# Routing rows normed early, experts gathered several at a time, a fifth raw buffer: one change to a two-layer decoder kernel

## The chip, the cores and the metric

The kernel runs on one core of a Trainium2 chip. The metric is the device time of one execution in microseconds (us). The engines are named as in the profile: PE is the matmul engine and PEld its weight loads, DVE the vector engine, ACT the scalar engine, POOL the GpSimd engine, and SP the engine that issues the DMAs. They run side by side and wait for each other by semaphores. PE's accumulators lie in PSUM, in eight banks of 128 x 512 floats.

## The reference

Two layers over 256 tokens of width 1024. Layer 0 is attention and a state space block followed by a dense feed-forward. Layer 1 is two kinds of attention followed by the part that the change touches, eight experts of which each token takes two:

```python
def moe_swiglu(h, router, w_gate, w_up, w_down):   # h: rms_norm(x, gain)
    logits = (t @ router).astype(jnp.float32)      # t: 256 x 1024, router: 1024 x 8
    top_val, top_idx = lax.top_k(logits, 2)
    top_w = jax.nn.softmax(top_val, axis=-1)
    ...   # out += gate of expert e * swiglu(t, w_gate[e], w_up[e], w_down[e])
```

`rms_norm` divides a row by its root mean square and multiplies by a gain for each column. `swiglu(h)` is `(silu(h @ gate) * (h @ up)) @ down`, with 2816 hidden columns.

## The kernel before

**Numbers in two halves.** Weights and activations are 32-bit floats. A matmul on the fast type (fp32r) keeps fewer digits, so `split` writes each 128 x 2048 weight tile `raw` as a rounded tile `wh` (ACT) and the rest `wl` (DVE, after ACT), and `mm3` (L513 to L517) issues three matmuls: high by high (L515), high by low (L516), low by high (L517).

**The order up to the routing's end** is made by `Recorder`: operations are recorded with their costs, planned over the engines under the number of buffers of each tile name (`RAW` for `raw`, 8 for PSUM), and then issued in that order. These instructions all carry line L326. `rec.late` marks operations of low urgency. After `rec.flush(...)` and `rec.on = False` the program is issued as it is written; those instructions carry L331.

**Routing.** For each of the two blocks b of 128 tokens, x3 (tile `xres`) is transposed by PE in pieces of 128 columns and multiplied by the router, in which the gain is folded (`rg`). The piece of x is the stationary operand and the 8 columns of the router are the moving one. x3 itself, not yet normed, is split into `xnh` and `xnl`. The logits give the two best experts by MAX8 and MAX_INDEX (`t8`, `i8`), the mask `m` and, with an exponential that needs the row scale `rows`, the weights `gate`. Two matmuls with triangular tables on `m` number the tokens of each expert (`posm`) and count them. The experts are then ordered by count: `poso` holds the positions in that order, `ids` the experts' numbers.

**Large and small.** The four fullest experts (`BIG = 4`; expert 0 is always the first) get 128 slots, the four others 64. `one_hots(p)` makes the one-hot tables of large expert p and small expert p. `gather` picks an expert's tokens out of xnh and xnl by multiplying with them, for 128 of the 1024 columns (index k) at a time. Four matmuls, of 128 + 64 = 192 columns where both experts are gathered together. The result is split into a tile pair `xb` (alternating between `fh` and `xg0`) for the large expert and kept whole in `xs` for the small. As the rows were not normed, `slot_scale` multiplies the tables with `rows` to get each slot's scale, used as `scale` in SiLU and in the product.

**Items.** The weights of an expert come in 11 chunks (`FC`) of three 1 MB units: gate and up, first half; gate and up, second half; down. A large chunk multiplies by `mm3`; a small one directly in 32 bits with the unsplit tile, two half arrays side by side. The list `items` starts with `LAG = 3` large chunks alone, then alternates large chunk g and small chunk g − 3, and ends with three small chunks alone. In item i, PE does the first gate and up unit of the item, transposes the hidden values of the item before, does the second unit, and then the down unit of the item before. The gather for large expert p + 1 and small expert p + 1 stands in the chunks c = 3 to 10 of expert p, one k in each; the tokens of small expert 0 are gathered in chunks 0 to 2 of expert 0.

**Loads.** `Stream` issues the units in order on SP, each into the next buffer that comes free: `RAW = 4` of the name `raw`, and `xres`, `xg0` (for loads up to `XG = 12`), `xg1`, `more` and `fl`. A buffer of a large unit is free when it has been split, one of a small unit when PE has used it. `st.ahead` splits up to `HL = 4` units ahead. Units of an expert other than the first need `ids`, which SP reads into a register.

Of the kernel before, what the change touches and what calls it, by code (L numbers as in the profile page):

```python
# [48 lines left out]
RAW = 4  # L49
# [3 lines left out]
XG = 12  # L53
BIG = 4
HALFP = 64
LAG = 3
PAIRED = 0.65
LATE, AFTER, HALF = 1, 2, 3
# [334 lines left out]
def kernel(ctx: ExitStack, tc: tile.TileContext, a, out: bass.AP):  # L393
# [379 lines left out]
    def ff_act(gu, scales, act=None):  # L773
        hs = []
        for b in range(len(gu)):
            si = tw(256)
            (act or tact)(si, gu[b][:, 0:256], AF.Silu, scale=scales[b])
            hh = tw(256)
            V.scalar_tensor_tensor(hh, gu[b][:, 256:512], scales[b], si, op0=OP.mult, op1=OP.mult)
            hs.append(hh)  # L780
        return hs
# [560 lines left out]
    rows, slots = mo([P, 2], "rows"), mo([P, 8], "slots")  # L1342
    for b in range(2):
        rx3 = rows[:, b:b + 1]
        lps = pa()
        for i in range(2):
# [24 lines left out]
        block_rstd(x3, b, rx3)  # L1371
# [9 lines left out]
        rec.late = 0  # L1381
    pp, pm = pa(), pa()
# [56 lines left out]
    def one_hots(p):  # L1439

        t = tw(dt=F32R).rearrange("p (b e s) -> p b e s", b=2, e=2)
        for b in range(2):
            one_hot(t[:, b, 0, :], (poso if p else posm)[:, b, p:p + 1])
            V.tensor_scalar(t[:, b, 1, :].rearrange("p (i s) -> p i s", i=2), bc(iota[:, None, 0:HALFP], [P, 2, HALFP]),
                            poso[:, b, BIG + p:BIG + p + 1], None, op0=OP.is_equal)
        return t

    oh = {0: one_hots(0)}


    def gather(k, ohs, xb=None, xs=None):

        lo, hi = 0 if xb else P, P + HALFP if xs is not None else P
        o = pa()[:, lo:hi]
        for i, src in enumerate((xnh, xnl)):
            for b in range(2):
                mmx(o, src[:, b, k * P:(k + 1) * P], ohs(b)[:, lo:hi], i + b == 0, i + b == 2)
        gain = k2("gf1k", k, k + 1)
        if xb:
            split_gain(xb[0][:, k], xb[1][:, k], o[:, 0:P], gain)  # L1460
        if xs is not None:
            S.activation(xs[:, k], o[:, P - lo:hi - lo], AF.Copy, scale=gain)

    def slot_scale(dst, ohs):

        sp, n = pa(), ohs.shape[2]
        for e in range(n):
            for b in range(2):
                mmx(sp[:, e:e + 1], ohs[:, b, e, :].bitcast(F32), rows[:, b:b + 1], b == 0, b == 1)
        V.tensor_copy(dst, sp[:, 0:n])  # L1470
# [30 lines left out]
    def large_tile(p):  # L1501
        t = mo([P, 2, 8, P], "xg0", F32R) if p % 2 else gtile([P, 2, 8, P], F32R, "fh")
        return t[:, 0], t[:, 1]

    def small_tile():
        return rec.tile(mo.pool, [P, 8, HALFP], F32, "mxs", 2, name="xs")
# [12 lines left out]
    def sm_act(gu, scale):  # L1519
        si, hh = tw(P), tw(P)  # L1520
        tact(si, gu[:, 0:P], AF.Silu, scale=scale)
        V.scalar_tensor_tensor(hh, gu[:, P:256], scale, si, op0=OP.mult, op1=OP.mult)
# [52 lines left out]
    xb, xs = {0: large_tile(0)}, {}  # L1575
    for k in range(8):
        gather(k, lambda b: oh[0][:, b].rearrange("p e s -> p (e s)"), xb[0])
    rec.late = AFTER
    slot_scale(slots[:, 0:2], oh[0])
    rec.late = 0  # L1580
    rec.flush([x3, oh[0], *xb[0], *st.tiles()])
    rec.on = False
    at.close()
    ov = out.rearrange("(b p) d -> p b d", p=P)
# [233 lines left out]
```

## Time and profile before

| what | value |
|---|---|
| median of 3 runs | 1165.53 us (1165.39 to 1167.24) |
| the profiled execution, its span | 1166.32 us, 1164.5 us |
| busy PE, PEld, DVE, ACT | 97%, 72%, 62%, 52% of the span |
| chain of work that ended last, by engine | PE 89%, DMA 5%, DVE 3%, ACT 1% |
| read from HBM | 345.95 MB, 298 GB/s over the span |
| split of weights on DVE, on ACT (128x2048, 90 each) | 206.4 us, 172.0 us |
| loads of expert units, issue to landing, median | 8.9 us into `raw` |

The first 450 us are the first layer and the second layer's attention; the routing ends at about 471 us and the experts fill the rest. PE is busy nearly always, and since its instructions overlap, a busy PE says little: what counts is how far apart matmuls start, and that is read from the timeline. DMA share and GB/s of a stretch say how near the loads are to their limit. In the chain of waits, each step is followed back to what released it. One execution is shown, and its stretches have different limits, so a saving is counted in the stretch where it is made.

### The profile page before, as it was taken

The page shows a single profiled execution, that of the slowest core. Times are in us where ns is not written, and L with a number is a line of the kernel's source. Part 1 is how long each engine was busy: PE and PEld are TensorE (multiplying, and loading weights), DVE is VectorE, ACT ScalarE, POOL GpSimd, SP SyncE. Part 2 cuts the span into 40 slices and gives each one's busy share as a digit, 9 for nine tenths or more (in the row PEclk, how much of TensorE's full clock was granted, in tenths as well). Part 3 has the DMA queues.
Part 4 walks back from the last instruction along what each step waited for, and adds up shares of the span by engine and source line. Part 5 has one row for each costly group of instructions (what it writes and reads, how often), then busy time and mean ns, then how long its engine had stood idle before and what let it go on. Part 6 is the DMA issues. An engine that isn't in the chain of part 4 may idle for free.

```text
span 1164.5 us, 16524 instructions
## 1 busy us (share of the span) xinstructions
PE 1133.4 (97%) x6143; PEld 833.2 (72%) x6143; DVE 720.7 (62%) x1185; ACT 601.2 (52%) x1016; POOL 28.7 (2%) x59
## 2 busy tenths in 40 slices
PE   6999999999999998999999999999999999999997
PEld 6887888888787777876666666666666666666663
DVE  5999954444399877665546565556565555565542
ACT  5768743444388565555445445554455444444331
POOL 1040000000300000000000000000000000000000
PEclk9999999999999998899999999999999999999999
DMA  9451565556344523489999999999999999999994
GB/s 348 154 190 73 183 214 186 188 182 220 112 160 163 194 73 145 176 330 356 401 414 415 419 377 409 395 423 420 393 419 389 420 382 406 411 410 420 415 415 156
DMA packets 52069, 348.13 MB, mean 299 GB/s; under 512 B 5904, under 2 KB 6032, under 8 KB 11536
## 3 DMA queue, kind: packets, MB, share of 16 engines
q1 hardware_dynamic: 51984, 347.02, 75.3%
q8 instruction: 50, 0.82, 0.3%
q14 instruction: 35, 0.29, 0.1%
HBM read 345.95 MB, written 1.05 MB: 298 GB/s over the span
## 4 chain that ended last, share of the span: by engine, by line
PE 89%; DMA 5%; DVE 3%; ACT 1%; issue 1%; SPq 0%; DVEq 0%; ACTq 0%
PE ps L331 24%; PE ps L515 19%; PE ps L517 18%; PE ps L516 18%; PE ps L326 10%; DMA raw<-in_moe_dram 2%; DMA fl<-in_moe_dram 1%; ACT wh L331 1%; DVE wl L326 1%; DMA raw<-in_w_dram 1%; DMA more<-in_moe_dram 1%; DVE wl L331 1%; DVE xres L331 0%; DVE tw L326 0%; DVE tw L331 0%
## 5 line engine op out<-in xcount | busy, mean ns | idle before, releaser
L331 DVE TENSOR_TENSOR wl<-raw,wh 128x2048 fp32r<-128x2048 f32 x90 | 206.4, 2293 | 156.5 <-ACT wh L331 156.5
L331 ACT ACTIVATE wh<-raw 128x2048 fp32r<-128x2048 f32 x90 | 172.0, 1911 | 110.3 <-DMA raw<-in_moe_dram 56.1
L515 PE MATMUL ps<-wh,fh 128*128 128x512 f32 (+2 forms) x544 | 220.4, 405 | 0.0
L516 PE MATMUL ps<-wl,fh 128*128 128x512 f32 (+2 forms) x544 | 211.4, 389 | 0.0
L331 ACT ACTIVATE tw<-ps 128x128 f32<-128x128 f32 (+2 forms) x114 | 43.6, 389 | 197.9 <-PE ps L331 195.9
L517 PE MATMUL ps<-wh,fl 128*128 128x512 f32 (+2 forms) x368 | 142.1, 386 | 0.0
L515 PEld LDWEIGHTS ps<-wh,fh 128*128 128x128 f32 x544 | 103.1, 189 | 20.0
L516 PEld LDWEIGHTS ps<-wl,fh 128*128 128x128 f32 x544 | 103.2, 190 | 17.6
L515 PE MATMUL ps<-wh,tw 128*128 128x512 f32 (+1 forms) x276 | 113.7, 412 | 0.7 <-ACT tw L326 0.7
L517 PE MATMUL ps<-wh,tw 128*128 128x512 f32 (+1 forms) x276 | 108.7, 394 | 0.0
L516 PE MATMUL ps<-wl,tw 128*128 128x512 f32 (+1 forms) x276 | 108.6, 394 | 0.0
L326 DVE TENSOR_TENSOR wl<-raw,wh 128x512 fp32r<-128x512 f32 (+1 forms) x149 | 98.4, 680 | 2.5 <-ACT wh L326 2.5
L331 DVE TENSOR_TENSOR tw<-ps,tw 128x256 fp32r<-128x256 f32 (+1 forms) x70 | 35.9, 521 | 97.5 <-ACT tw L331 97.4
L331 PE MATMUL ps<-raw,xs 128*64 128x256 f32 x720 | 87.2, 384 | 0.0
L326 ACT ACTIVATE wh<-raw 128x512 fp32r<-128x512 f32 (+1 forms) x130 | 74.8, 628 | 18.2 <-PE ps L517 10.0
L517 PEld LDWEIGHTS ps<-wh,fl 128*128 128x128 f32 x368 | 69.1, 188 | 14.6 <-DVE fl L326 0.4
L515 PEld LDWEIGHTS ps<-wh,tw 128*128 128x128 f32 x276 | 51.9, 188 | 26.8 <-issue 15.4
L515 PE MATMUL ps<-wh,xg 128*128 128x512 f32 x176 | 71.0, 403 | 0.0
L517 PE MATMUL ps<-wh,fh 128*128 128x512 f32 x176 | 69.8, 397 | 0.0
L331 PEld LDWEIGHTS ps<-raw,xs 128*64 128x64 f32 x720 | 48.4, 136 | 29.8 <-issue 8.2
L517 PE MATMUL ps<-wh,xg 128*128 128x512 f32 x176 | 69.3, 394 | 0.0
L516 PE MATMUL ps<-wl,xg 128*128 128x512 f32 x176 | 68.7, 390 | 0.0
(296 smaller groups left out, 1767.9 us busy)
## 6 DMA issues: line engine op xcount, KB each, us to landing
raw<-in_moe_dram SPq DMA_DIRECT2D x131, 1024.0 KB, 8.9
xg<-in_moe_dram SPq DMA_DIRECT2D x33, 1024.0 KB, 8.6
xres<-in_moe_dram SPq DMA_DIRECT2D x33, 1024.0 KB, 8.2
more<-in_moe_dram SPq DMA_DIRECT2D x32, 1024.0 KB, 8.5
fl<-in_moe_dram SPq DMA_DIRECT2D x32, 1024.0 KB, 8.5
raw<-in_ffn_dram SPq DMA_DIRECT2D x30, 1024.0 KB, 4.7
raw<-in_w_dram SPq DMA_DIRECT2D x23, 1024.0 KB, 5.0
raw<-in_ffn_dram SPq DMA_DIRECT2D x12, 256.0 KB, 3.6
```

What stands on the lines that cost most here:

```text
L326: return (self.name, self.cost(fn, args, kw), lambda: real(*args, **kw))
L331: return getattr(self.eng, fn)(*args, **kw)
L515: nc.tensor.matmul(ps, xh, wh, start=start, stop=False)
L516: nc.tensor.matmul(ps, xh, wl, start=False, stop=False)
L517: nc.tensor.matmul(ps, xl, wh, start=False, stop=stop)
```

## The change

Six things are changed. **(1)** The row scale is computed ahead of the split, and `split_gain` writes xnh and xnl already normed. `slot_scale` and the scales in SiLU and its product are gone. **(2)** In the logits the router is the stationary operand, so the result is 8 x 128 and is copied, transposed and copied again. **(3)** Ten 512-column matmuls (`WARM`) are issued into an unused accumulator after the logits. **(4)** The first large expert is gathered alone as before; the four small experts are gathered together (4 x 64 = 256 columns) in the first four chunks, large experts 1 and 2 together (256 columns) in chunks 6 to 9 of expert 0, and large expert 3 (128 columns) in chunks 2 to 5 of expert 1, two k in each chunk. Large results are kept whole in `xl` (tile `xg0`) and split in one piece into `fh` after the last chunk of the expert before (`large_split`). **(5)** The tables for the scatter are made one chunk ahead of their transposes. **(6)** `RAW` is 5, `XG` 14 and `LAG` 4.

```diff
-RAW = 4
+RAW = 5
-XG = 12
+XG = 14
-LAG = 3
+LAG = 4
+WARM = 10
...
     for b in range(2):
         rx3 = rows[:, b:b + 1]
+        block_rstd(x3, b, rx3)
         lps = pa()
...
-                T.matmul(lps[:, 0:8], xt[:, kk * P:(kk + 1) * P], rg[:, 4 * i + kk, :], start=i + kk == 0,
+                T.matmul(lps[0:8, 0:P], rg[:, 4 * i + kk, :], xt[:, kk * P:(kk + 1) * P], start=i + kk == 0,
                          stop=i == 1 and kk == 3)
-            flex(xnh[:, b, cs], x3[:, b, cs])
-            V.tensor_tensor(xnl[:, b, cs], x3[:, b, cs], xnh[:, b, cs].bitcast(F32), OP.subtract)
+            split_gain(xnh[:, b, cs], xnl[:, b, cs], x3[:, b, cs], rx3)
+        lt = tw(P, 8)
+        V.tensor_copy(lt, lps[0:8, 0:P])
+        lps = pa()
+        T.transpose(lps[:, 0:8], lt, ident[0:8, 0:8])
...
-        block_rstd(x3, b, rx3)
...
+    idle = pa()
+    rec.late = AFTER
+    for i in range(WARM):
+        mmx(idle, u3r[:, 0:P], xnh[:, 1, 0:512], True, True)
+    rec.late = 0
...
+    def gather_split(k, ohs, x):
+        o, gain = gather(k, ohs, P)
+        split_gain(x[0][:, k], x[1][:, k], o, gain)
+
+    def gather_all(k, oh, dst):
+
+        n, w = oh.shape[2], oh.shape[3]
+        o, gain = gather(k, lambda b: oh[:, b].rearrange("p e s -> p (e s)"), n * w)
+        S.activation(dst[:, :, k], o.rearrange("p (e s) -> p e s", e=n), AF.Copy, scale=gain)
...
+    def large_split(src):
+        x = large_tile()
+        S.activation(x[0], src, AF.Copy)
+        V.tensor_tensor(x[1], src, x[0].bitcast(F32), OP.subtract)
+        return x
...
-            hs[it] = sm_act(gu, slots[:, e:e + 1]) if sm else ff_act([gu], [slots[:, e:e + 1]])
+            hs[it] = sm_act(gu) if sm else ff_act([gu])
+            if not sm and c == FC - 1 and p < BIG - 1:
+                xb = large_split(xl[:, p % 2])
...
+            for k in range(2 * c, 2 * c + 2):
+                gather_all(k, oh_s, xs)
+        if p == 0 and LAG + 2 <= c < LAG + 6:
+            if c == LAG + 2:
+                xl, oh_l = mo([P, 2, 8, P], "xg0"), one_hots(1, 2)
+            for k in range(2 * (c - LAG - 2), 2 * (c - LAG - 1)):
+                gather_all(k, oh_l, xl)
+        if p == 1 and 2 <= c < 6:
+            if c == 2:
+                oh_l = one_hots(3, 1)
+            for k in range(2 * c - 4, 2 * c - 2):
+                gather_all(k, oh_l, xl[:, 0:1])
```

In the issued order three places matter. (In the changed kernel the helper lines stand one line lower.) The first is PE between the logits and the first gather. `tw` are work tiles, here the transposed x, the router, the logits, the triangular table u3r and the one-hot tables; `cp` holds the identity. Before:

```order
L326 MATMUL ps<-cp,xres 128x128
L326 MATMUL ps<-tw 128x8 x9
L326 MATMUL ps<-m,tw 128x8
L326 MATMUL ps<-m,tw 128x16
L326 MATMUL ps<-m,tw 128x8 x2
L326 MATMUL ps<-tw,xnh 128x128 x5
L326 MATMUL ps<-tw,xnl 128x128 x2
```

And after:

```order
L327 MATMUL ps<-tw 8x128 x9
L327 MATMUL ps<-cp,tw 128x8
L327 MATMUL ps<-xnh,tw 128x512
L327 MATMUL ps<-cp,tw 128x8
L327 MATMUL ps<-xnh,tw 128x512 x9
L327 MATMUL ps<-m,tw 128x8
L327 MATMUL ps<-m,tw 128x16
L327 MATMUL ps<-m,tw 128x8 x2
L327 MATMUL ps<-tw,xnh 128x128 x5
```

The two small transposes of the logits and the ten 512-column matmuls now stand between the logits and the matmuls on `m`, one of the ten ahead of the second transpose.

The second place is ACT in the same stretch, from the sum of squares of block 1 (`ssx`) to the first gathered tile `fh`; `rs` is the row scale on its way and `e` the exponential. Before:

```order
L326 ACTIVATE tw,ssx<-xres 128x1024
L326 ACTIVATE tw<-ps 128x512
L326 ACTIVATE rs_r_3303<-ssx,eps 128x1
...
L326 ACTIVATE e_3307<-d_3306,rows 128x1
L326 ACTIVATE e_3325<-d_3324,rows 128x1
L326 ACT_TABLE_LOAD
L326 ACTIVATE fh<-ps,c_2873 128x128 x8
```

And after:

```order
L327 ACTIVATE wh<-raw 128x512
L327 ACTIVATE xnh<-xres,rows 128x512 x2
L327 ACTIVATE e_3328<-d_3327,rows 128x1
L327 ACTIVATE e_3308<-d_3307,rows 128x1
L327 ACT_TABLE_LOAD
L327 ACTIVATE fh<-ps,c_2873 128x128 x8
```

The two pieces of xnh of block 1, which stood earlier and read x3 alone, now read `rows` and stand just ahead of the exponentials.

The third place is PE in a pair of the first expert that holds a piece of the gather; `xs` is the small expert's tokens, the other operand of its matmuls a loaded weight tile. Before, at chunk 3:

```order
L331 MATMUL ps<-rows,tw 128x1 x4
L331 MATMUL ps<-tw,xnh 128x192 x2
L331 MATMUL ps<-tw,xnl 128x192 x2
L331 MATMUL ps<-raw,xs 64x256 x8
L331 MATMUL ps<-cp,tw 128x128 x2
L331 MATMUL ps<-raw,xs 64x256 x8
```

And after, at chunk 8:

```order
L332 MATMUL ps<-fl,tw 64x512 x4
L332 MATMUL ps<-tw,xnh 128x256 x2
L332 MATMUL ps<-tw,xnl 128x256 x2
L332 MATMUL ps<-tw,xnh 128x256 x2
L332 MATMUL ps<-tw,xnl 128x256 x2
L332 MATMUL ps<-raw,xs 64x256 x8
L332 MATMUL ps<-cp,tw 128x128 x2
```

The slot scales are gone, and a pair that gathers has eight matmuls of 256 columns where it had four of 192.

## Rows read from the trace of the kernel before

**Rows 1.** Stretches: us, then busy PE, PEld, DVE, ACT, POOL, clock, DMA, GB/s

```profile
466.00:523.00 57.00, 57.00 (x284) 46.78 (x285) 36.30 (x50) 30.74 (x40) 0.00 (x0) 0.91 0.69 258
...
650.00:690.00 40.00, 40.00 (x223) 27.44 (x218) 24.58 (x26) 20.06 (x22) 0.00 (x0) 1.00 1.01 420
...
1003.00:1124.00 121.00, 118.03 (x644) 78.80 (x642) 67.40 (x56) 55.26 (x58) 0.00 (x0) 1.00 1.01 417
```

**Rows 2.** Timeline of PE (start, us, what), two down units with gathers between

```profile
568.72 1.94 PE L331 MATMUL ps<-more,tw 128*64 128x512 f32 x8
...
583.96 1.94 PE L331 MATMUL ps<-raw,tw 128*64 128x512 f32 x8
```

**Rows 3.** Timeline of PE, the same place in two pairs without gathers

```profile
1064.61 1.94 PE L331 MATMUL ps<-more,tw 128*64 128x512 f32 x8
...
1079.07 1.94 PE L331 MATMUL ps<-raw,tw 128*64 128x512 f32 x8
```

**Rows 4.** Waits after 500 us: who waited for whom, us, times, longest

```profile
PE ps L331 <- DVE tw L331: 3.1, 6, 1.1
```

**Rows 5.** Timeline of PE in the routing; idle time before and releaser in brackets

```profile
456.12 2.37 PE L326 MATMUL ps<-tw 128*128 128x8 f32 x18
461.03 1.01 PE L326 MATMUL ps<-m,tw 128*128 128x8 f32 x4 [2.53 <-DVE m L326]
462.85 1.30 PE L326 MATMUL ps<-tw,xnh 128*128 128x128 f32 x5 [0.81 <-DVE rank L326]
...
469.71 1.81 PE L326 MATMUL ps<-rows,tw 128*128 128x1 f32 x8
471.38 0.77 PE L515 MATMUL ps<-wh,fh 128*128 128x512 f32 x1
...
476.53 0.40 PE L515 MATMUL ps<-wh,fh 128*128 128x512 f32 x1
```

**Rows 6.** Stretches with the granted clock: three of the routing, one earlier

```profile
458.00:459.00 1.00, 0.49 (x5) 0.40 (x4) 1.00 (x8) 0.00 (x0) 0.00 (x0) 1.00 0.08 25
...
460.00:461.00 1.00, 0.00 (x0) 0.00 (x0) 1.00 (x8) 0.98 (x2) 0.00 (x0) 0.50 0.00 0
...
477.00:478.00 1.00, 1.00 (x6) 0.84 (x5) 0.00 (x0) 1.00 (x1) 0.00 (x0) 1.00 0.00 0
...
366.00:368.00 2.00, 0.34 (x2) 0.00 (x0) 1.97 (x11) 2.00 (x6) 0.00 (x0) 1.00 0.42 70
```

**Rows 7.** Timeline of PE at full clock, a 256-column matmul and 512-column ones

```profile
369.33 0.28 PE L517 MATMUL ps<-wh,tw 128*128 128x256 f32 x1
369.44 0.39 PE L515 MATMUL ps<-wh,tw 128*128 128x512 f32 x1
369.67 0.40 PE L516 MATMUL ps<-wl,tw 128*128 128x512 f32 x1
```

**Rows 8.** Timelines of ACT and DVE in the routing

```profile
454.56 1.06 ACT L326 ACTIVATE tw<-xres 128x1024 bf16<-128x1024 f32 x1
...
459.52 0.70 ACT L326 ACTIVATE e<-d,rows 128x1 f32<-128x1 f32 x2 [1.53 <-DVE d L326]
...
455.03 0.68 DVE L326 TENSOR_TENSOR xnl<-xres,xnh 128x512 fp32r<-128x512 f32 x1
...
461.02 0.15 DVE L326 TENSOR_TENSOR m<-sel,sel 128x8 fp32r<-128x8 f32 x1
...
467.37 0.35 DVE L326 SCALAR_TENSOR_TENSOR fh<-ps,c,fh 128x128 fp32r<-128x128 f32 x1 [0.37 <-ACT fh L326]
```

**Rows 9.** Timeline of PE, slot scales of the second expert pair

```profile
508.68 0.95 PE L331 MATMUL ps<-rows,tw 128*128 128x1 f32 x8
509.49 0.45 PE L331 MATMUL ps<-tw,xnh 128*128 128x192 f32 x2
```

**Rows 10.** Chain of waits that ended last (start, us, what), one round apart

```profile
646.34 6.36 PE ps L331 x44
...
817.15 6.36 PE ps L331 x44
```

More of the change, by code (lines that the diff above doesn't have):

```diff
@@ L1448, with both_halves @@
[L1448 to L1454, printed above, removed]
+            V.tensor_tensor(t[:, b], bc(iota[:, None, 0:width], [P, n, width]),
+                            bc(poso[:, b, lo:lo + n, None], [P, n, width]), OP.is_equal)
+        return t
+    def both_halves(r):
+        t = tw(256, dt=F32R).rearrange("p (b s) -> p b s", b=2)
+        for b in range(2):
+            V.tensor_scalar(t[:, b].rearrange("p (i s) -> p i s", i=2), bc(iota[:, None, 0:HALFP], [P, 2, HALFP]),
+                            poso[:, b, r:r + 1], None, op0=OP.is_equal)
+        return t
@@ L1455, in gather @@
+    oh0 = tw(256, dt=F32R).rearrange("p (b s) -> p b s", b=2)
+    for b in range(2):
+        one_hot(oh0[:, b], posm[:, b, 0:1])
+    def gather(k, ohs, n):
+        o = pa()[:, 0:n]
         for i, src in enumerate((xnh, xnl)):
             for b in range(2):
[L1457 to L1470, printed above, removed]
+                mmx(o, src[:, b, k * P:(k + 1) * P], ohs(b), i + b == 0, i + b == 2)
+        return o, k2("gf1k", k, k + 1)
+    def gather_split(k, ohs, x):
+        o, gain = gather(k, ohs, P)
+        split_gain(x[0][:, k], x[1][:, k], o, gain)
@@ L1574 @@
                        [(place("xg1"), 999), (place("more"), 999), (place("fl"), 999)]), whole)
[L1575 removed]
+    xb = large_tile()
     for k in range(8):
[L1577 to L1581, printed above, removed]
+        gather_split(k, lambda b: oh0[:, b], xb)
+    rec.flush([x3, *xb, *st.tiles()])
     rec.on = False
     at.close()
+    top = scope("t")
+    xs = top([P, BIG, 8, HALFP], "xs")
+    oh_s = one_hots(BIG, BIG, HALFP)
     ov = out.rearrange("(b p) d -> p b d", p=P)
[L1585 removed]
+    ys, ohs, ohts, hs, pend = {}, {}, {}, {}, None
     N = len(items)
@@ L1619 @@
             continue
+        if c == 0:
+            ohs[sm] = both_halves(BIG + p) if sm else one_hots(p, 1)[:, :, 0]
         if c == 1:
-            ohts[sm] = oht_of(*(oh[p][:, b, int(sm), :] for b in range(2)))
+            ohts[sm] = oht_of(ohs[sm][:, 0], ohs[sm][:, 1])
         if sm:
             continue
-        both = lambda b, q: oh[q][:, b].rearrange("p e s -> p (e s)")
         if p == 0 and c < LAG:
-            if c == 0:
-                xs[0] = small_tile()
-            for k in range(c * 3, min(8, c * 3 + 3)):
-                gather(k, lambda b: both(b, 0), None, xs[0])
-        if p < BIG - 1 and c == 2:
-            oh[p + 1] = one_hots(p + 1)
-        if p < BIG - 1 and c >= LAG:
-            if c == LAG:
-                xb[p + 1], xs[p + 1] = large_tile(p + 1), small_tile()
-                slot_scale(slots[:, 2 * p + 2:2 * p + 4], oh[p + 1])
-            gather(c - LAG, lambda b: both(b, p + 1), xb[p + 1], xs[p + 1])
+            for k in range(2 * c, 2 * c + 2):
[10 more added lines that the diff above has]
+                gather_all(k, oh_l, xl[:, 0:1])
     scatter(*pend)
```

43 lines of the change are left out of this document (20 added, 23 removed).

## Prediction

> **What bounds the kernel now.** I read the busy times by stretch first. From about 523 us to the end the matmul engine is busy all the time and the loads run at almost full share: 420 GB/s in the best long stretch, 417 GB/s late, but only 258 GB/s between 466 and 523 us [rows 1]. So in the expert stage two things are near their limit, and I next asked which one ends last. The lengths of pairs answer it. A pair is one chunk of a large expert and one of a small one, six loads of 1.0486 MB. A pair with a piece of the gather takes 583.96 − 568.72 = 15.24 us, one without it 1079.07 − 1064.61 = 14.46 us [rows 2, 3]. The loads of a pair take 6.29 MB / 420 GB/s = 14.98 us. With a gather PE is the slower one, without it the loads are. The waits agree: PE waited for the loads' consumers only 3.1 us in all after 500 us [rows 4], which lie in the last expert round, the one without a gather.
>
> The other place is the routing, between the attention's last matmul and the first expert. PE issues 18 records of logits from 456.12 to 458.5, stands idle for 2.53 us until DVE has the mask m, idles again for 0.81, then gathers from 462.85 to 469.71, computes the slot scales until 471.38 and only then starts the first expert [rows 5]. The granted clock is 1.00 until 459, 0.50 at 460, and 1.00 again from 477 [rows 6]: these are its levels of 2.4 and 1.2 GHz. The first twelve expert matmuls, from 471.38 to 476.53, start 0.43 us apart [rows 5], where 512 columns at the upper level take 0.23 [rows 7]. The clock fell within a microsecond or two of the last logits matmul, behind a run of transposes and 8-column matmuls, and came back some 5 us after the first expert's matmuls began.
>
> **The change part by part, routing.** All sums are made against the profiled execution, 1166.32 us (span 1164.5), which is 0.8 above the median 1165.53.
>
> Rows normed ahead of their split: rows (the root mean square) of block 1 must now be there before xnh and xnl. The two DVE instructions for xnl are no dearer (0.68 each [rows 8]), but the order puts them ahead of MAX_INDEX and the selections, 2 × 0.61 = 1.2 us on the path to m. On ACT the two xnh pieces stand ahead of the two exponentials, behind which m is queued already now: the exponentials end at 460.22, m at 461.17 [rows 8]. Logits with the router stationary: as many matmuls, with 128 moving columns in place of 8. A record takes 2.37 / 18 = 0.13 us now [rows 5]; one that streams 128 columns I put at no less than the 0.11 of a 256-column one [rows 7], so from 0 to −0.6 us in all, of which little is on the path because ACT's copies pace it. New is the way back: a copy, a transpose, a copy, each small (a DVE one on 8 columns takes 0.15 [rows 8]); with the handovers some 0.6 us. Together m comes 1.8 us later (0.6 to 3.0).
>
> The slot scales go: 8 records, 471.38 − 469.71 = 1.67 us off the path. The ten dummy 512-column matmuls stand between logits and mask counts. They need only xnh and fill what was idle: 10 × 0.23 = 2.3 us. One of them stands ahead of the second block's small transpose, so that transpose, and the copy and MAX8 behind it, wait for xnh. That is inside the 1.8.
>
> What they are worth is the clock. If it stays at 2.4 GHz: the 32 gather matmuls go from 6.86 to 3.4 us, the four counting matmuls from 1.0 to 0.5, and the first twelve expert matmuls from 476.53 − 471.38 = 5.15 to 12 × 0.23 = 2.75. At that pace the gather is led by DVE, which writes 8 × 0.35 us of fl halves and ten small instructions of 0.13 in between; I add 0.6. Sum with the clock up: +1.8 − 1.7 − 3.4 − 0.5 − 2.4 + 0.6 = **−5.6 us**. Sum with the clock down as now: +1.8 − 1.7 = **0**. All of this moves PE's start, and PE leads until well after 523 us since the loads idle there [rows 1]; so it moves the end.
>
> **The change, expert stage.** Gathers before: a pair with one is 0.78 us longer, 8 pairs in each of three rounds, and slot scales of 0.81 us once in each [rows 2, 3, 9]: 24 × 0.78 + 3 × 0.81 = 21.1 us. After: four pairs with 8 matmuls of 256 columns, four with 8 of 128. A 256-column matmul takes 0.11 us [rows 7]; for 128 columns no row at full clock has these operands, so I bound it by half the 0.21 that the first expert's 128-column gather takes at the lower level (6.86 / 32), 0.11, and by 0.12. With 0.15 for the seams that is 1.1 us a pair, 8.8 in all. The small experts' gather is 32 matmuls in either kernel, 0.11 to 0.12 each, +0.3. PE's work falls by **12.0 us**.
>
> Whether it can be had depends on the loads. The chain of waits passes the same place of two rounds at 646.34 and 817.15 [rows 10]: a round is 171 us. Without gather and slot scale it is 171 − 8 × 0.78 − 0.8 = 164.0 of PE. Its 66 loads, 69.2 MB, take 164.8 us at 420 GB/s and 166.0 at 417. So:
> - round 0: PE leads in both (168 against 165): 7.0 becomes 4.4, −2.6
> - round 1: the same, −2.6
> - round 2: from 171 to the loads' 164.8 plus 0.5 for seams, −5.7
> - round 3: no gather in either; now 164.0 + 3.1 of waits = 167.1, afterwards 165.3, −1.8. This rests on the fifth raw buffer: one more load can be queued, which is what a stretch of stalls at 417 GB/s lacks; without it 0.
>
> With +0.3 the sum is **−12.4 us**. Ends: loads at 417 and no help from the buffer, −2.6 − 2 − 5 + 0 = −9.5; PE leading everywhere, −2.6 − 2.6 − 7 − 3.1 = −15.3.
>
> The rows decide the ceiling here. The Trainium skill, DMA: Bandwidth & Descriptors, "Where 436 GB/s comes from", puts 435.2 GB/s on the SBUF ports and says that for HBM to SBUF about 358 a core binds. The trace goes against the second figure with its 420. By 435.2 a pair's loads would take 14.46 us, and rounds 2 and 3 would reach the −15.3 end.
>
> What costs nothing: scales dropped from SiLU and from its product make ACT and DVE instructions shorter, both lie under PE's matmuls. The one-piece split at a round's end is 1.06 us of ACT (by the 1024-element square [rows 8]) and about as much of DVE; PE has other work then, a small chunk and a large down projection, 14.46 less the 24 matmuls of 0.23 of the gate and up halves, 8.9 us. LAG 4 exchanges a pair for one large and one small chunk alone, within 0.2 us. The tail of small chunks alone has 12 loads instead of 9; three loads take 7.5 us and a small chunk on PE about 6 (14.46 less 36 matmuls of 0.23), so it uses up 2 us more of the loads' lead, and costs 2 us if there is none.
>
> **The rivals.**
> 1. *The clock falls all the same.* For it: after the dummies PE again has about 3 us with only four small matmuls, and then a gather of short ones; the fall at 459 came behind such a stretch. Against: the dummies are dense and end 1 to 1.5 us before the counts; from 366 to 368 PE was busy for 0.34 us alone and the clock stayed at 1.00 [rows 6]. Price: routing 0 instead of −5.6. 1165.5 − 12.4 = **1153** (1150 to 1156). The Trainium skill, TensorE: Matmul & The Clock Gate, "Part 4: PE-mode transpose", says that a transpose does not count as PE activity; by that the 19 transposes ahead of the logits help no more than now, and this rival gains weight. The trace, where the clock fell behind them, does not contradict it.
> 2. *Round ends stall.* ACT and DVE are in order; if the one-piece split stands behind a split that waits for its load, PE stands at three seams, an estimated 3 us each (the split's two steps and a handover) where the 8.9 us are used up, with the buffer giving nothing: −5.6 − 9.5 + 9 = −6, **1159.5**. Against it: PE's waits come to 3.1 us in the whole stage [rows 4].
> 3. *Slower: the loads set the end and the routing is longer.* The loads that need the experts' numbers restart when ids is written, behind m on DVE. That comes 1.8 to 3 us later, and if the stage followed the loads from there, the end would move by as much: **1168**. It decides if the loads run without a gap from ids on. Against it: 258 GB/s until 523 [rows 1], and 13 loads instead of 11 are issued ahead of ids.
> 4. *The change does its work, but loads eat it:* clock up, −5.6 − 9.5, **1150.5**. It is the upper end of the forecast.
>
> **How the numbers follow.** Forecast: −5.6 − 12.4 = −18.0 on 1165.5, **1147.5**; its own range 1143 (−22.5, with −15.3 and 2 us less of routing delay) to 1151.5. Chances: forecast with rival 4, 0.50; rival 1, 0.32; rival 2, 0.08; rival 3, 0.05; a mixture that cancels, 0.05. The range of 8 in 10 reaches from 1143 to 1157: it takes in the forecast and rival 1 and leaves out 2 and 3. About 0.2%, 2.3 us, is what a measurement of this kernel can tell from no change: faster 0.91, same 0.03, slower 0.06.
>
> **What would show it.** Routing: the granted clock at 1.00 through the gather, m about 2 us later, first expert matmul near 468 us. If the clock is 0.50 there, rival 1. Rounds: places one round apart 168, 168, 165 us instead of 171; a pair of 15.5 us for eight pairs only, and others between 14.5 and 15.1. If GB/s in rounds 2 and 3 stays at 417 and PE's waits grow beyond 5 us, the loads ate it. A gap on PE ahead of the first matmul of experts 1 to 3 would show rival 2. The forecast is wrong if the first expert starts later than now, or if rounds stay at 171.

## The result, and the profile of the changed kernel

The changed kernel takes 1151.91 us (median of 4, 1151.45 to 1152.93), the kernel before 1165.46 in the same comparison: a ratio of 0.9891, with an interval from 0.9875 to 0.9906. That is 13.6 us faster. The forecast was 1147.5 with a range of 1143 to 1157. The profiled execution took 1151.45 us, its span 1149.7 against 1164.5.

| what | before | after |
|---|---|---|
| span of the profiled execution | 1164.5 us | 1149.7 us |
| m written, end of the last instruction | 461.17 us | 463.21 us |
| first matmul of the first expert; the thirteenth | 471.38; 476.53 us | 470.56; 474.63 us |
| the other 14.8 - 1.9 us | | 12.9 us, in the expert stage |

First the routing. This is the timeline of PE in the changed kernel (start in us, length, what it is; in brackets the idle time ahead and what ended it), to be held against [rows 5]:

```profile
456.76 2.13 PE L327 MATMUL ps<-tw 128*8 128x128 f32 x18
...
459.00 0.49 PE L327 MATMUL ps<-xnh,tw 128*128 128x512 f32 x1
...
459.71 2.34 PE L327 MATMUL ps<-xnh,tw 128*128 128x512 f32 x9
463.14 0.68 PE L327 MATMUL ps<-m,tw 128*128 128x8 f32 x4 [1.10 <-DVE e L327]
465.00 0.74 PE L327 MATMUL ps<-tw,xnh 128*128 128x128 f32 x5 [1.17 <-DVE rank L327]
...
470.56 0.73 PE L516 MATMUL ps<-wh,fh 128*128 128x512 f32 x1
...
474.63 0.39 PE L516 MATMUL ps<-wh,fh 128*128 128x512 f32 x1
```

The ten 512-column matmuls fill 459.0 to 462.0, but idle stretches of 1.10 and 1.17 us are left on either side of the four counts. The granted clock (last but two of the columns of the stretches, as in [rows 6]) shows what came of it:

```profile
465.00:466.00 1.00, 1.00 (x9) 1.00 (x10) 1.00 (x4) 0.00 (x0) 0.00 (x0) 1.00 0.00 0
467.00:468.00 1.00, 1.00 (x6) 1.00 (x6) 0.88 (x5) 0.51 (x2) 0.00 (x0) 0.50 0.33 98
...
474.00:475.00 1.00, 1.00 (x6) 0.82 (x5) 0.00 (x0) 0.17 (x1) 0.00 (x0) 1.00 0.00 0
```

The clock held through the counts and the first third of the gather, then fell to 0.50 with PE busy, and was back by 474. Before it had been down from 460 to 477. So the gather takes 470.56 - 465.00 = 5.56 us where it took 6.86, and the first twelve expert matmuls 4.07 where they took 5.15.

Then the expert stage: two of the stretches of [rows 1] and a longer one (us, then busy PE, PEld, DVE, ACT, POOL, clock, DMA share, GB/s), then what PE waited for after 500 us, to be held against [rows 4]:

```profile
466.00:523.00 57.00, 57.00 (x283) 46.38 (x283) 43.07 (x59) 35.70 (x41) 0.00 (x0) 0.94 0.67 252
...
1003.00:1124.00 121.00, 120.83 (x683) 79.57 (x681) 62.24 (x59) 49.32 (x57) 0.00 (x0) 1.00 1.01 420
...
750.00:1080.00 330.00, 329.83 (x1804) 219.86 (x1798) 193.21 (x171) 155.56 (x166) 0.00 (x0) 1.00 1.01 421
...
PE ps L332 <- DVE tw L332: 1.4, 4, 0.6
```

From 750 to 1080 us PE is busy for 329.83 of 330 us and the loads run at full share as well. Neither waits for the other in a way that costs. The same place one round apart, the second unit of small chunk 8 on PE's timeline, and after it the small chunk's down unit in two pairs with a gather and in two without:

```profile
640.21 1.08 PE L332 MATMUL ps<-raw,xs 128*64 128x256 f32 x8
...
809.18 1.08 PE L332 MATMUL ps<-more,xs 128*64 128x256 f32 x8
...
972.80 1.08 PE L332 MATMUL ps<-xg,xs 128*64 128x256 f32 x7
...
559.70 1.94 PE L332 MATMUL ps<-fl,tw 128*64 128x512 f32 x8
...
575.44 1.94 PE L332 MATMUL ps<-raw,tw 128*64 128x512 f32 x8
...
1060.02 1.51 PE L332 MATMUL ps<-more,tw 128*64 128x512 f32 x6
...
1074.46 1.94 PE L332 MATMUL ps<-xg,tw 128*64 128x512 f32 x8
```

In the kernel before, one unit of a small chunk, again one round apart:

```profile
633.54 0.65 PE L331 MATMUL ps<-raw,xs 128*64 128x256 f32 x4
...
804.37 0.87 PE L331 MATMUL ps<-fl,xs 128*64 128x256 f32 x6
...
975.50 0.87 PE L331 MATMUL ps<-xg,xs 128*64 128x256 f32 x6
```

Rounds take 168.97 and 163.62 us where they took 170.83 and 171.13; a pair takes 15.74 with a gather and 14.44 without. Last, the chain of waits (start, us, what), which runs through the loads from 729 us on and, but for the output's last steps, through PE alone from 1034 us to the end:

```profile
729.12 9.91 DMA xres<-in_moe_dram
...
741.40 2.21 DVE wl L332
743.62 11.37 DMA xres<-in_moe_dram
...
1031.91 2.20 DVE wl L332
1034.50 2.31 PE ps L332 x18
...
1112.25 24.94 PE ps L332 x173
```

Read alone, this chain says that the loads set the end. It follows the loads back because a split starts as its load lands. That the split's product then lies ready for 3 us or more, and PE does not wait, a chain doesn't show. Which of the two sets the end, the experiments on the expert stage had to tell.

### The profile page after: what moved, and what is told of

It reads as the page before. It is cut to its first block, busy times and chain, and to the rows that moved or that the text cites. A ratio compares the mean times of both kernels' runs of the same rounds, so it can differ in the third digit from the quotient of the medians.

```text
span 1149.7 us, 16360 instructions
## 1 busy us (share of the span) xinstructions
PE 1121.7 (98%) x6091; PEld 825.0 (72%) x6091; DVE 713.0 (62%) x1170; ACT 588.5 (51%) x987; POOL 29.0 (3%) x59
## 4 chain that ended last, share of the span: by engine, by line
PE 68%; DMA 19%; DVE 7%; ACT 4%; issue 1%; SPq 0%; ACTq 0%; DVEq 0%
DMA xres<-in_moe_dram 18%; PE ps L516 15%; PE ps L518 15%; PE ps L517 15%; PE ps L332 14%; PE ps L327 10%; DVE wl L332 4%; ACT wh L332 4%; DMA raw<-in_w_dram 1%; DVE wl L327 1%; DVE xres L332 0%; DVE tw L327 0%; DVE tw L332 0%; SPq L446 0%; DVE more L327 0%
## 5 line engine op out<-in xcount | busy, mean ns | idle before, releaser
L516 PE MATMUL ps<-wh,fh 128*128 128x512 f32 (+2 forms) x720 | 290.3, 403 | 0.0
L517 PE MATMUL ps<-wl,fh 128*128 128x512 f32 (+2 forms) x720 | 279.7, 388 | 0.0
L332 ACT ACTIVATE tw<-ps 128x128 f32<-128x128 f32 (+2 forms) x202 | 72.9, 363 | 320.1 <-PE ps L332 288.6
L516 PEld LDWEIGHTS ps<-wh,fh 128*128 128x128 f32 x720 | 135.9, 189 | 28.1
L517 PEld LDWEIGHTS ps<-wl,fh 128*128 128x128 f32 x720 | 136.0, 189 | 23.9
L332 DVE TENSOR_TENSOR tw<-ps,tw 128x256 f32<-128x256 f32 (+3 forms) x158 | 66.7, 427 | 137.1 <-ACT tw L332 136.9
L518 PE MATMUL ps<-wh,fh 128*128 128x512 f32 x352 | 138.3, 393 | 0.0
L332 DVE TENSOR_TENSOR wl<-xres,wh 128x2048 fp32r<-128x2048 f32 x39 | 89.2, 2288 | 46.1 <-ACT wh L332 46.1
L332 PE MATMUL ps<-raw,xs 128*64 128x256 f32 x960 | 116.3, 384 | 0.0
L332 ACT ACTIVATE wh<-xres 128x2048 fp32r<-128x2048 f32 x39 | 74.8, 1918 | 55.6 <-DMA xres<-in_moe_dram 53.2
L518 PEld LDWEIGHTS ps<-wh,fh 128*128 128x128 f32 x352 | 66.3, 188 | 14.5
```

The source lines that it names most:

```text
L332: return getattr(self.eng, fn)(*args, **kw)
L516: nc.tensor.matmul(ps, xh, wh, start=start, stop=False)
L517: nc.tensor.matmul(ps, xh, wl, start=False, stop=False)
L518: nc.tensor.matmul(ps, xl, wh, start=False, stop=stop)
```

## Experiments on the routing and the clock

The start of the program varies by up to 2.7 us between executions: the row at 424.97 in the kernel before (`ps<-cp,more`, in the second layer's attention; called the early row below) stands anywhere from 423.2 to 426.0. So the table counts from that row to the counts on m, and from these to the thirteenth expert matmul, in the one execution of each version that was profiled. The changed kernel and the four versions below that share its routing agree in both numbers within 0.1 us, and in all five the clock fell inside the gather. The medians come from several comparisons, in which the kernel before took 1164.1 to 1165.5 us.

| version | to the counts | counts to thirteenth | sum | median, us |
|---|---|---|---|---|
| before | 36.06 | 15.50 | 51.56 | 1165.46 |
| changed | 38.25 | 11.49 | 49.74 | 1151.91 |
| w0: no extra matmuls | 38.94 | 13.53 | 52.47 | 1154.41 |
| logit: logits as before | 37.46 | 12.64 | 50.10 | 1152.70 |
| w0_logit: both | 37.22 | 12.29 | 49.51 | 1151.63 |
| fill: twenty, in the planner's order | 43.15 | 8.17 | 51.32 | 1152.60 |
| hold: twelve, spread | 38.24 | 14.09 | 52.33 | 1152.95 |
| hold2: three blocks, 6, 9, 5 | 39.76 | 7.87 | 47.63 | 1148.35 |
| hold3: three blocks, 6, 6, 5 | 39.05 | 7.90 | 46.95 | 1147.87 |

**Without the ten extra matmuls.**

```diff
-WARM = 10
+WARM = 0
```

> The changed kernel without the ten 512-column matmuls (WARM = 0); nothing that the outputs need is left out. Theory A (the ten keep the clock up for the counts and the first third of the gather, and PE leads from the first expert to the end): the clock is back at 0.5 before the counts, the gather takes 6.9 us in place of 5.56, the first expert's matmuls run at 0.43 us spacing until some 5 us after they start, the end is 1.5 to 2.5 us later than the changed kernel's, profiled span 1151.2 to 1152.2 against 1149.7. Rival (the gather is led by DVE and the logits' way back is shorter without them): first expert matmul within 0.3 us of 470.56, span within 0.5 us of 1149.7.

Measured: 1154.41 us (1153.62 to 1155.54), ratio 0.9908 (0.9890 to 0.9926), span 1153.3, 1.1 above the upper end of what was expected. The clock fell ahead of the counts and stayed down:

```profile
461.00:462.00 1.00, 0.00 (x0) 0.00 (x0) 1.00 (x5) 0.56 (x2) 0.00 (x0) 1.00 0.84 352
463.00:464.00 1.00, 0.00 (x0) 0.00 (x0) 1.00 (x7) 0.98 (x2) 0.00 (x0) 0.82 0.00 0
465.00:466.00 1.00, 0.18 (x2) 0.13 (x2) 0.96 (x7) 0.00 (x0) 0.00 (x0) 0.50 0.71 254
```

From the counts to the thirteenth expert matmul it takes 2.0 us more, which is what theory A gave the ten; another 0.7 is lost ahead of the counts, where the planner ordered DVE otherwise (`rows` is there only at 460.0 us, in the changed kernel at 458.2). That the loss was seen in the end, 2.5 us by the medians and 2.0 by the ratios, says that what happens in the routing does move the end.

**Both idle stretches filled.**

```diff
+    rec.late = AFTER
+    for i in range(5):
+        mmx(idle, u3r[:, 0:P], xnl[:, 1, 512:1024], True, True)
...
+    for i in range(5):
+        mmx(idle[0:16, :], mf, xnh[:, 1, 0:512], True, True)
```

> The changed kernel with five more 512-column matmuls behind the ten (they read the last piece of xnl, so they cannot start before it) and five that read m ahead of the gather, so that both idle stretches of PE in the routing are filled. Theory A (the clock falls because PE idles for 1.1 and 1.2 us around the counts): the granted clock is 1.00 through the gather, the gather takes about 4 us in place of 5.56, the first twelve expert matmuls 2.8 us in place of 4.1, and the end is 2.5 us earlier, span near 1147.2 if the first 450 us stay as they are. Rival (the short matmuls of the gather bring the clock down whatever stands ahead of them): 0.5 during the gather all the same, span 1149.5 to 1150.5.

Measured: 1152.60 us (1151.09 to 1156.42), span 1150.8. The mechanism bears theory A out: the clock stayed at 1.00 through the gather, and counts to thirteenth matmul took 475.63 - 467.46 = 8.17 us in place of 11.49. But the planner answered the ten further instructions with another order of the whole front, and the counts began at 467.46 in place of 463.14:

```profile
459.18 3.22 PE L327 MATMUL ps<-tw 128*8 128x128 f32 x28 [1.01 <-ACT tw L327]
...
467.46 0.61 PE L327 MATMUL ps<-m,tw 128*128 128x8 f32 x4 [0.33 <-DVE d L327]
467.94 1.10 PE L327 MATMUL ps<-xnh,m 128*16 128x512 f32 x4
468.88 0.58 PE L327 MATMUL ps<-tw,xnh 128*128 128x128 f32 x4
...
472.89 0.39 PE L516 MATMUL ps<-wh,fh 128*128 128x512 f32 x1
```

3.3 us were won and, counted from the early row, 4.9 lost. In this order the clock was lost elsewhere: PE idled for 4.29 us ahead of 371.39 us, and the clock stood at 0.50 from 371 to 376, so that the mean clock of the execution is 0.995 all the same. A mean clock alone doesn't say where the clock was lost. The next three versions keep the changed kernel's order ahead of the routing.

**Twelve extra matmuls where PE idles, and the tables one chunk early.**

```diff
-WARM = 10
+WARM = 4
...
+    for i in range(4):
+        mmx(idle, u3r[:, 0:P], xnl[:, 1, 512:1024], True, True)
...
+    for i in range(4):
+        mmx(idle[0:16, :], mf, xnh[:, 1, 0:512], True, True)
...
+        if p == 0 and c == LAG + 1:
+            oh_l = one_hots(1, 2)
...
+        if p == 1 and c == 1:
+            oh_l = one_hots(3, 1)
```

> The changed kernel with twelve extra matmuls in place of ten, put where PE idles: four that read xnh, four that read the last piece of xnl, and four that read m, between the counts and the gather; the order of the first 452 us on PE stays that of the changed kernel, which the version with both idle stretches filled did not keep. And the one-hot tables of large experts 1 to 3 are made one chunk ahead of their gather. Theory A (idle PE around the counts brings the clock down): clock 1.00 through the gather, from the counts to the twelfth expert matmul 8.2 us in place of 11.5, so 3.3 us earlier; the early tables take away the two waits of 0.62 and 0.50 ahead of the first gather of a group, 1.1 us. Together 4.4 us, span 1145.3. Rival (PE has only 8 of the 12 on time, the clock falls as in the changed kernel): 1.1 us alone, span 1148.6.

Measured: three executions of 1152.91 to 1153.05 us at a mean clock of 0.992, and one of 1146.05 at 0.999; span of the profiled one 1151.1. The trace shows one of the first three: PE idles ahead of the counts for 1.62 us, longer than in the changed kernel, and the clock was lost there:

```profile
460.69 1.09 PE L327 MATMUL ps<-xnl,tw 128*128 128x512 f32 x4
463.40 0.98 PE L327 MATMUL ps<-m,tw 128*128 128x8 f32 x4 [1.62 <-DVE d L327]
...
465.00:466.00 1.00, 1.00 (x4) 0.56 (x3) 1.00 (x8) 0.00 (x0) 0.00 (x0) 0.50 0.65 131
```

The execution that kept the clock has a span of 1144.3, near theory A's 1145.3; the three others are 2.5 us above the rival's 1148.6, as in the trace the clock fell just ahead of the counts and not in the gather. The difference, some 7 us between executions of the same instructions, is for the most part the price of the clock in this routing: from the counts to the thirteenth matmul it takes 14.09 us here and 7.90 in the last version of the table, where the clock held. The start of the program can have a share in the rest. The early tables did what they should: the waits of 0.62 and 0.50 us ahead of the first gather of each group are gone, and the distance to the changed kernel shrinks there by 0.8 and 0.6 us.

**Three blocks that leave the order alone.** Each block of extra matmuls is recorded as a single operation of almost no cost, so that the planner does not move anything for it. The order is then that of w0, without extra matmuls. The tables are made early as in the version before.

```diff
...
+    keep(idle, u3r[:, 0:P], xnh[:, 1, 512:1024], 6)
+    keep(idle, u3r[:, 0:P], xnl[:, 1, 512:1024], 9)
...
+    keep(idle[0:16, :], mf, xnh[:, 1, 0:512], 5)
```

> The changed kernel with the extra matmuls issued in three blocks that leave the rest of the order alone: six on xnh behind both small transposes of the logits, nine on the last piece of xnl, which is there only at 461.0 us, and five on m behind the counts; and the one-hot tables one chunk early. Theory A (idle PE ahead of and behind the counts brings the clock down; with twelve extra matmuls three executions of four still lost it, at a mean clock of 0.992, and the one that kept it, 0.999, took 1146.05 us): with both stretches filled most executions keep the clock, mean clock 0.999, 1145 to 1147 us, span 1143.5 to 1145. Rival (chance decides whatever stands there): executions at 1146 and at 1151 to 1153 side by side, as with hold.

Measured: 1148.35 us (1148.00 to 1150.78), ratio 0.9874 (0.9858 to 0.9891), mean clock 0.998 in all four executions, span 1146.4. The counts stand behind the nine, and from the first of the three blocks on PE isn't idle until the expert:

```profile
463.07 2.20 PE L1396 MATMUL ps<-xnl,tw 128*128 128x512 f32 x9
465.11 0.50 PE L327 MATMUL ps<-m,tw 128*128 128x8 f32 x4
465.48 1.32 PE L1396 MATMUL ps<-xnh,m 128*16 128x512 f32 x5
466.63 0.67 PE L327 MATMUL ps<-tw,xnh 128*128 128x128 f32 x5
...
470.15 0.45 PE L516 MATMUL ps<-wh,fh 128*128 128x512 f32 x1
```

The gather takes 3.52 us and counts to thirteenth 7.87. The end came later than expected by 1.4 to 2.9 us, since m was late again (the counts 39.76 behind the early row, 1.5 more than in the changed kernel, of which w0's order makes 0.7). Ahead of the first block PE is still idle for 1.28 us, and the clock held: an idle stretch of that length doesn't bring it down in every place.

> The version with three blocks of extra matmuls, with six in place of nine in the second block: there m is written at 464.40 us and its counts start at 465.11, behind the last of the nine. Theory A: the counts start 0.7 us earlier behind m, the clock stays at 1.00, the span falls by 0.7 against that version's 1146.4, to 1145.7, and the median is near 1147.6. Rival (with three fewer the clock falls in some executions): executions near 1152 at a mean clock of 0.992 to 0.995.

With six in place of nine: 1147.87 us (1145.74 to 1149.40), ratio 0.9862 (0.9846 to 0.9879), span 1144.0. The counts start 0.7 us earlier behind the early row, as expected. Two executions ran at a mean clock of 0.999 and two at 0.996; where these two lost it no trace shows, so whether three matmuls fewer carry a risk stays open. This version has the lowest median, within the noise of the one with nine. It is 4.0 us below the changed kernel by the medians and 3.4 by the ratios to the kernel before (the two intervals just touch); 1.4 of it comes from the early tables. Against w0, which has the same order, the three blocks are worth 13.53 - 7.90 = 5.6 us from the counts to the thirteenth matmul.

**The logits as before**, with and without the ten.

```diff
-                T.matmul(lps[0:8, 0:P], rg[:, 4 * i + kk, :], xt[:, kk * P:(kk + 1) * P], ...
+                T.matmul(lps[:, 0:8], xt[:, kk * P:(kk + 1) * P], rg[:, 4 * i + kk, :], ...
...
-        lt = tw(P, 8)
-        V.tensor_copy(lt, lps[0:8, 0:P])
-        lps = pa()
-        T.transpose(lps[:, 0:8], lt, ident[0:8, 0:8])
```

> The changed kernel with the logits as before: the piece of x stationary, 8 router columns moving, no way back through a copy and a transpose. By the prediction m comes about 0.6 us earlier for the handovers saved, and the logits matmuls take about as long. If the clock stays up through the ten dummies as in the changed kernel, the span falls by 0 to 0.6, 1149.1 to 1149.7. Rival (matmuls of 8 columns let the clock fall, those of 128 hold it): the clock is at 0.50 before or during the dummies, the routing is 1 to 2 us longer, span 1150.7 to 1151.7.

> The changed kernel without the ten extra matmuls and with the logits as before (8 columns moving). Tells apart what held the clock until 463.6 us in the version without the ten. If it is the 128 columns of the changed logits: the clock falls at 459 to 460 here, as in the kernel before. If it is something else in the new order: at 463 to 464 again. The span is then 1151 to 1153.3 in either case, since the gather runs at 0.50 in both.

Measured: 1152.70 us (1149.85 to 1152.92) with the ten, 1151.63 us (1149.87 to 1153.67) without. First the clock with the ten, then without:

```profile
459.00:460.00 1.00, 1.00 (x6) 0.82 (x5) 1.00 (x5) 0.17 (x1) 0.00 (x0) 0.99 0.23 33
461.00:462.00 1.00, 1.00 (x3) 0.33 (x1) 1.00 (x8) 0.66 (x3) 0.00 (x0) 0.50 1.01 426
```

```profile
459.00:460.00 1.00, 0.00 (x0) 0.00 (x0) 1.00 (x7) 0.22 (x2) 0.00 (x0) 0.50 1.04 434
```

In the first trace, with 8 moving columns, the clock is down at 460 though the ten 512-column matmuls have been running since 458.61; in the second it fell between 457 and 458. With 128 columns it was still at 1.00 at 462 with no extra matmul at all (w0). In these executions, then, the clock held some 4 us longer behind the wider logits, and the ten prolonged that. It isn't shown for every execution: two of the four with the ten ran at a mean clock of 0.992, as the profiled one did, but two at 0.994, like the changed kernel.

The wider logits cost 0.8 us to the counts with the ten (38.25 against 37.46) and 1.7 without (38.94 against 37.22). And the ten are worth their 2.0 us behind the counts only together with the wider logits; with the logits as before nothing is seen of them (12.64 with, 12.29 without). The span of 1148.0 without the ten is 3 us below the lower end of what was expected: 1.3 us of that were there at the early row, and the clock was back by 472, in w0 only by 478. Taken together, extra matmuls and turned logits gain nothing that can be measured: 1151.63 us and a ratio of 0.9902 (0.9885 to 0.9918) without both, 1151.91 and 0.9891 (0.9875 to 0.9906) with both.

## Experiments on the expert stage

**Gathers of large experts done twice.**

```diff
                 gather_all(k, oh_l, xl)
+                gather_all(k, oh_l, xl)
...
+                gather_all(k, oh_l, xl[:, 0:1])
                 gather_all(k, oh_l, xl[:, 0:1])
```

> The changed kernel with each piece of the gather of large experts 1 to 3 done twice: 64 more matmuls, 32 of 256 columns and 32 of 128, in eight pairs. Theory B (PE leads from the first expert to the end, the loads run beside it with a lead that they use up slowly): each of the eight pairs about 1 us longer and the end 7.5 to 8.5 us later than the changed kernel's, span 1157.2 to 1158.2. Rival (the loads set the end from 726 us on, where the chain of waits goes through them): what is added in rounds 0 and 1 is caught up behind, the end 0 to 4 us later, span below 1154.

Measured: 1159.49 us (1159.07 to 1160.49), 7.6 more than the changed kernel. Two down units, one pair apart:

```profile
578.12 1.94 PE L332 MATMUL ps<-raw,tw 128*64 128x512 f32 x8
...
594.82 1.94 PE L332 MATMUL ps<-raw,tw 128*64 128x512 f32 x8
```

The pair takes 16.70 us in place of 15.74. Eight such pairs make about the 7.6 us by which the end is later, so all of it arrives there: PE's work in rounds 0 and 1 is on the path.

**Less work for PE in round 2.** The low-by-high matmuls of the gate and up halves are left out for large expert 2 (`lean` is set there alone).

```diff
+        elif lean:
+            nc.tensor.matmul(ps, xh, wh, start=start, stop=False)
+            nc.tensor.matmul(ps, xh, wl, start=False, stop=stop)
...
+            lean[:] = [1] if not sm and p == 2 else []
...
```

> The changed kernel without the low-by-high matmuls of the gate and up halves of large expert 2 (in round 2): 88 matmuls of 512 columns, 88 x 0.23 = 20.2 us of PE, are left out; all loads and splits stay. Theory B with the lead as it is (the loads run at full rate from about 700 us on at 14.87 us a pair against PE's 14.44, and the last landing stands 8 us before PE's end): the loads become the bound within a few pairs, PE waits for most of the 20 us, and the end moves by 1 to 5 us, span 1145 to 1148.7. Rival (the loads have much to spare): the end 15 to 20 us earlier, span below 1135.

Measured: 1152.45 us (1151.51 to 1153.12), 0.5 more than the changed kernel, which is within the noise. 20.2 us of PE's work were gone, and nothing of it was seen:

```profile
750.00:1080.00 330.00, 311.42 (x1716) 204.16 (x1714) 192.55 (x171) 153.44 (x166) 0.00 (x0) 1.00 1.01 421
...
PE ps L332 <- DVE tw L332: 11.8, 10, 1.3
PE ps L332 <- ACT tw L332: 7.2, 9, 1.8
```

PE waited 19.0 us instead, and the loads ran at 421 GB/s as they do in the changed kernel. Even the 1 to 5 us that theory B still gave were too much. So from round 2 on the loads are at their limit as well as PE: less work on PE brings nothing there. More work on PE was tried in rounds 0 and 1 alone, and there it costs its full time.

**One buffer fewer in the changed kernel, and the fifth buffer alone in the kernel before.**

```diff
-RAW = 5
+RAW = 4
```

> The changed kernel with RAW = 4, one buffer fewer. Theory B with the lead as the trace shows it (a first-half unit lands 11 us ahead of its split in round 1 and 4 us ahead in round 3): one load of 2.5 us less lead leaves some pairs of the last round waiting, waits of 1 to 3 us in all, span 1150.7 to 1152.7; the prediction gave the buffer 1.8 us. Rival (the lead is not needed): span within 0.5 us of 1149.7.

> The kernel before with the fifth raw buffer alone (RAW = 5). Theory B (before, PE led rounds 0 to 2 by its gathers, so that the loads had time to keep up, and waited 3.1 us in round 3): only those waits can go, 2 to 3.1 us, span 1161.4 to 1162.5 against 1164.5; the prediction gave it 1.8. Rival (the buffer is worth what it is worth in the changed kernel, 6.6 us by the medians): span 1158.

Measured for the first: 1158.52 us (1156.54 to 1160.18), 6.6 more, and more than any side expected. For the second: 1163.33 us (1161.77 to 1164.10), ratio to the kernel before 0.9987 (0.9976 to 0.9997), 1.5 us by the medians; its span 1161.0 is 3.5 shorter, of which 1.2 was there already at the early row. First the changed kernel with four, then the kernel before with five:

```profile
750.00:1080.00 330.00, 324.89 (x1762) 217.49 (x1758) 190.13 (x170) 152.25 (x163) 0.00 (x0) 1.00 1.01 417
...
PE ps L332 <- DVE tw L332: 6.8, 11, 1.2
```

```profile
PE ps L331 <- DVE tw L331: 0.4, 2, 0.3
PE ps L331 <- ACT tw L331: 0.4, 1, 0.4
```

In the kernel before, the buffer took away the 3.1 us of waits [rows 4] and left 0.4; the rest of the stage is PE's own time. In the changed kernel it is worth some four times as much: with four buffers the loads move 417 GB/s, with five 421, and PE waits for 7.9 us in all in place of 1.8. That PE's shorter gathers no longer leave the loads time to catch up is the reading of this, not a measurement. The buffer and the other edits are worth more together than alone: by the medians 6.9 us without the buffer, 1.5 for the buffer by itself, 13.6 together.

**LAG of 3.**

```diff
-LAG = 4
+LAG = 3
...
-            for k in range(2 * c, 2 * c + 2):
+            for k in range(3 * c, min(8, 3 * c + 3)):
```

> The changed kernel with LAG = 3: three large chunks alone ahead of the pairs and three small ones alone at the end (the small experts' gather in three pieces a chunk). By the prediction LAG is worth within 0.2 us on PE, and four chunks alone use 2 us more of the loads' lead at the end: span within 0.5 us of 1149.7. Rival (the longer start alone is where the loads get ahead: units land early while PE works without small chunks): without it the lead is short, PE waits in the last round as with four raw buffers, 2 to 4 us later.

Measured: 1153.83 us (1152.33 to 1154.92), ratio 0.9911 (0.9895 to 0.9928), 1.9 more by the medians; PE waited 3.3 us after 500 us in place of 1.8. That fits the rival at its lower end, by which the fourth large chunk alone gives the loads a longer start. But the interval overlaps with the changed kernel's, and the pieces of the gathers move with LAG, so the cause isn't settled.

## Why the prediction was right, and where it was wrong

**The size.** 13.6 us were measured where 18.0 were forecast. The range held the time because it reached to rival 1, and rival 1 is nearer to what happened (1153) than the forecast.

**The step that failed is the clock through the gather.** The text took the ten matmuls for dense enough and the 1 to 1.5 us behind them for too short to matter. The clock fell in the gather, and the routing moved by -1.9 us at the thirteenth expert matmul, not by -5.6. With both idle stretches beside the counts filled and w0's order otherwise, it did not fall (hold2, hold3); which of the two brings it down isn't shown, as they were filled only together. By its terms, from the rows of both kernels: m and the counts +2.1 (1.8 forecast), from the counts to the gather 0 (-0.5; PE waits for DVE's `rank` in both kernels), slot scales -1.7 as forecast, the gather -1.3 (-3.4 + 0.6), the first twelve matmuls -1.1 (-2.4). Had the clock held, the forecast's terms were about right: in hold3 the second half, counts to thirteenth matmul, is 15.50 - 7.90 = 7.6 us shorter than before, and the forecast's terms for it add up to 7.4.

**The delay of m** came as worked out, and the parts can now be told apart: 1.2 us for the normed rows (37.22 against 36.06; 1.2 forecast for the two DVE instructions ahead of the selections) and 1.0 for the turned logits and the ten (38.25 against 37.22; 0.6 forecast).

**The transposes.** The same 16 transposes (the text says 19) stand ahead of the logits in w0 and w0_logit, and counted from the early row the clock was lost some 4 us apart. What differs between the two is the form of the logits, with its way back. The prediction put the Trainium skill, TensorE: Matmul & The Clock Gate, "Part 4: PE-mode transpose", by which a transpose "doesn't count as PE-busy the same way", on the side of rival 1; no run here tests that by itself.

**The expert stage** gave 12.9 us, 12.4 were forecast, but not by the forecast's steps:

- *The gather's price was too low.* A pair with 256 columns costs 15.74 - 14.44 = 1.3 us more and one with 128 columns 15.63 - 14.44 = 1.2, where 1.1 was put for both; the tables made in the chunk of their first use cost two waits of 0.62 and 0.50 us, which the text did not have. PE's work falls by some 10 us (21.1 less four pairs of each kind and the two waits), not 12.0; with the 3 us of other waits that went, that makes the 12.9 nearly.
- *The loads' ceiling was put too low.* Round 2 was to take 165.3 us, 0.5 above the loads' 164.8; it took 163.6, what PE needs. At 421 GB/s the 69.2 MB take 164.4; that a round slower by 0.8 on the loads' side costs nothing as long as buffered units last fits the version with one buffer fewer, but wasn't measured by itself. Round 1 gained 1.9 (2.6 forecast), round 2 7.5 (5.7 forecast), and 3.5 are left for rounds 0 and 3 with the small experts' gather (4.1 forecast). About 358 GB/s a core, which the Trainium skill, DMA: Bandwidth & Descriptors, "Where 436 GB/s comes from", gives as the limit of the HBM side, is again not what the trace shows, with 421.
- *The fifth buffer and LAG were given too little.* 1.8 us were forecast for the buffer, in round 3 and in itself; in the changed kernel it is worth 6.6, since without it the gathers' gain doesn't reach the end. LAG was given 0.2 and may be worth 1.9. That the sum came out within 0.5 us is luck: PE's work fell by 2 us less than was put, and the waits and the loads' ceiling gave as much more.

**Rivals 2 and 3** did not come. No gap of PE stands ahead of the first matmul of experts 1 to 3: its longest wait after 500 us is 0.6 us, ahead of a gather. The later m and ids did not make the end later: the span is shorter by 14.8 us. Rival 4, loads that eat the gain, is in kind what the version with four buffers shows.

**Two sums** of the prediction are slightly off, without consequence: the low end of the expert stage adds up to -9.6 and not -9.5, the early end of the forecast's own range to -22.9 and not -22.5.

## What to carry to other kernels

Where two engines are near their limits, a saving on one reaches the end only with the buffers that let the other keep its pace: try the size of the ring with every such edit, and judge the ring together with it and not alone. A chain of waits that runs through loads is no proof that they set the end; take work from the other side and look. Matmuls that are there for the clock alone are to be put right up to the real work on both sides of a short step: ten in one block lost the clock in the gather, three blocks, of six, nine and five, kept it in four executions of four. In a kernel whose order is planned they should not cost the planner anything, and whether they earn more than the delay they bring has to be measured.

## What the runs showed of the hardware that was not expected

- The granted clock fell to 0.50 inside the gather, with PE busy, between 466 and 467 us, after two idle stretches of 1.1 and 1.2 us, the second of which ended at 465.0. In one traced execution it fell under running 512-column matmuls where the logits ahead of them had 8 columns (0.99 at 459 to 460, 0.50 at 461 to 462).
- It held through an idle stretch of 1.28 us where three blocks of 512-column matmuls followed without a gap.
- The same instructions ran at a mean clock of 0.992 in three executions and 0.999 in one, 7 us apart (hold).
- With a fifth raw buffer the changed kernel's loads moved 421 GB/s in place of 417, in a stretch where the DMA share was 1.01 in both.
- At a granted clock of 1.00, gather matmuls of 256 columns started 0.117 us apart (0.94 us for eight, 1.3 with the seams), those of 128 columns 0.11.
